# Forgetting attention of a two-layer decoder: gates projected beside the values, running sums brought back from DRAM as bias tiles, scores on each head's own 64 rows

## Chip, cores and metric

One core of one Trainium2 chip runs the whole program in one launch. The metric is the device time of one launch in microseconds (us); lower is better. Three runs of the kernel before were timed: 756.55, 757.05 and 758.76 us, median 757.05 us.

## The reference, cut to what matters

The program computes two decoder layers on 256 tokens of width 1024 in float32. Layer 0 mixes by dilated attention (three patterns), layer 1 by forgetting attention; each is followed by a SwiGLU network. The change touches layer 1's attention alone: 16 heads of 64, and for every head one gate per token, whose log-sigmoid is summed along the tokens. The difference of two sums is added to each score.

```python
def forgetting_mixer(h, w_in, b_f, w_out):
    proj = h @ w_in                                   # 3 * 1024 columns of q, k, v and 16 of gates
    ...
    log_f = jax.nn.log_sigmoid(proj[..., 3 * ATTN_WIDTH:] + b_f)
    c = lax.cumsum(log_f, axis=1)                     # 256 tokens x 16 heads
    ...
        s = jnp.einsum('bihd,bjhd->bhij', qi, k) * scale
        s = s + ci[..., None] - ck[:, :, None, :]
        s = jnp.where(key_pos[None, :] <= qpos[:, None], s, NEG_INF)
        p = jax.nn.softmax(s, axis=-1)
        return jnp.einsum('bhij,bjhd->bihd', p, vf)
    ...
    return o @ w_out
```

The term `ci` is the same for all keys of a query, and a softmax doesn't see it; the kernels add the running sum of the key alone.

## The kernel before

Every large product is made of three TensorE matmuls (`mm3`): both operands are split into a high and a low part, and high by high, high by low and low by high are summed in PSUM. The high part is a rounded copy that ScalarE (ACT) makes, the low part the difference, which VectorE (DVE) makes (`split`, L73 and L75). Weights come in pieces of 128x2048 numbers: two transfers of 512 KB each into `raw` (five buffers), issued by the queue of SyncE (SP), and two splits into `wh` and `wl` (four buffers each, by pieces). A transfer can start when DVE has split the piece five transfers earlier, and a split when TensorE (PE) is through with the piece four earlier.

The Tile scheduler fixes the order of the instructions on each engine when the program is built; at run time each engine takes its own list from the front and waits where an operand or a buffer isn't there. Two tools steer the order: `first()` raises the priority of what is within it, and a table of due work, filled by `later(i, fn, ...)` and read after each step i of the projection loop (and at its middle, i - 0.5), says at which step attention work is written down.

The attention of layer 1 works on four quads of four heads. The list `b_units` gives 12 projection steps: for a quad, q (w = 0), k (w = 1) or the values (w = 2). A step of q or k is 48 matmuls of 256 columns. The values of quads 0 and 1 are made in one pair (`proj_pair`, 512 columns a matmul), those of quad 2 beside them (`proj_tok`), and this first block is written out by hand: tokens 0 to 127 (t = 0), then tokens 128 to 255 (t = 1), whose transposed activations `norm_t` makes in the middle of the block. Then come steps 3 to 11 in a loop: q and k of quad 0 (steps 3 and 4), of quad 1 (5 and 6), and so on. For each pair of heads `scores_b` makes the scores, adds the mask, and does the softmax; `trans_b` and `pv_b` follow one or two steps later.

The gates go their own way. `gates_1` projects them with eight matmuls of 512 columns, `softplus` transposes them and starts `log1p` (about 15 small DVE instructions on 128x32 numbers, with one power on GpSimd, POOL, after the second). `gates_2` transposes the result back on PE and makes the running sum with a scan on DVE (L816). The scores get it by a longer contraction: q and k of a head lie in `qz` and `kz`, with 16 more rows (`aux`), where `kz` holds the running sums of all heads and `qz` a column that picks the head's own (`sel`, copied on POOL, L901). So the score matmuls (L832) contract over 80 or 128 rows, and `maskb` is the same for all heads.

Of the kernel before, what the change touches and what calls it, by code (L numbers as in the profile page):

```python
# [16 lines left out]
P = 128  # L17
# [14 lines left out]
def trunk(ctx: ExitStack, tc: tile.TileContext, T, out):  # L32
# [5 lines left out]
    ps = ctx.enter_context(tc.tile_pool(name="ps", bufs=1, space=bass.MemoryType.PSUM))  # L38

# [67 lines left out]

    a_units = []
# [5 lines left out]
    b_units = [(0, 2), (1, 2), (2, 2), (0, 0), (0, 1), (1, 0), (1, 1), (2, 0), (2, 1), (3, 0), (3, 1), (3, 2)]  # L114
# [650 lines left out]
    aux = (slice(64, 64 + NH), slice(0, NH))
    qz, kz = ([ap.tile([P, 2, S], F32, tag=f"fm{w}", name=f"z{w}", bufs=2) for _ in range(2)] for w in range(2))
    for y in qz[1], kz[1]:
        nc.gpsimd.memset(y[:64], 0.0)

    def gates_1():  # L770

        o = psum("o")
        for k in range(KT):
            nc.tensor.matmul(o[:32 + NH].rearrange("p (x s) -> p x s", x=2), wf[:, k, :32 + NH], xt.full[:, k],
                             start=k == 0, stop=k == KT - 1)
        z, u = gt[:NH, :S], gt[:NH, S:]
        with first():
            nc.scalar.activation(u, o[32:32 + NH, :S], AF.Copy)
            nc.vector.scalar_tensor_tensor(z, o[:NH, :S], bf, u, op0=ALU.add, op1=ALU.add)
            nc.vector.tensor_tensor(z, z, o[:NH, S:], op=ALU.add)  # L780

    def softplus():

        z = gt[:NH, :S]
        tr = psum("tr")
        for t in range(2):
            nc.tensor.transpose(tr[:, t * NH:(t + 1) * NH], z[:, t * P:(t + 1) * P], ident[:NH, :NH])
        with first():
            log1p(tr)

    def log1p(tr):
        zt, m, t, s, w, a = (ga[:, i, :] for i in range(6))
        nc.vector.tensor_copy(zt, tr[:, :2 * NH])

# [13 lines left out]
    def gates_2():  # L808

        tr = psum("tr")  # L810
        for t in range(2):
            nc.tensor.transpose(tr[:NH, t * P:(t + 1) * P], ga[:, 1, t * NH:(t + 1) * NH], ident)
        cs, one = gt[:NH, :S], gt[:NH, S:]
        with first():
            nc.vector.memset(one, 1.0)
            nc.vector.tensor_tensor_scan(cs, one, tr[:NH, :S], 0.0, op0=ALU.mult, op1=ALU.add)  # L816
            for h in range(2):
                nc.vector.tensor_copy(kz[h][aux[h]], cs[:, None, :].to_broadcast([NH, 2, S]))
# [4 lines left out]
    def scores_b(hq, pr):  # L823
# [4 lines left out]
        rows = (slice(0, 64 + NH), ALL)  # L828
        scs = [psum("sc") for _ in range(2)]
        for h in range(2):  # L830
            for qb in range(2):
                last = nc.tensor.matmul(scs[h][:, qb * P:qb * P + (qb + 1) * P],  # L832
                                        qz[h][rows[h], pr, qb * P:(qb + 1) * P],
                                        kz[h][rows[h], pr, :(qb + 1) * P], start=True, stop=True)
# [31 lines left out]
    ws = [weights("b_in", b_units[i][0] * 3 + 2) for i in range(2)]  # L866
    os = [psum("mm") for _ in range(2)]
    vs = [v_tile() for _ in range(2)]
    for i in range(2):
        bq[i][2] = vs[i]  # L870
        proj_pair(xt, ws[i], os, i, (0,))
    v_pair(vs, os[0], 0)
    w2, o2 = weights("b_in", b_units[2][0] * 3 + 2), psum("sc")
    proj_tok(xt, w2, o2[:, :S], 0, hook=(2, lambda: norm_t(*hs[1], g_b, xt, 1)))
    for i in range(2):
        last = proj_pair(xt, ws[i], os, i, (1,))
        with tc.issue_after(last.ins):
            (gates_1, softplus)[i]()
    v_pair(vs, os[1], 1)
    proj_tok(xt, w2, o2[:, S:], 1)  # L880
    bq[2][2] = v_tile(o2)
    later(4, gates_2)
    for i, (hq, w) in enumerate(b_units):
# [4 lines left out]
        if w < 2:  # L888
# [9 lines left out]
            for h in range(2):  # L898
                if w == 0:
                    pick = sel[aux[h], hq * 4 + h:hq * 4 + h + 3:2]  # L900
                    nc.gpsimd.tensor_copy(qz[h][aux[h]], pick[:, :, None].to_broadcast([NH, 2, S]))  # L901
                nc.scalar.activation((qz, kz)[w][h][own[h]], o[own[h]].rearrange("p (a b) -> p a b", a=2), AF.Copy,
                                     scale=(0.125, 1.0)[w])
# [63 lines left out]
def _constants():  # L967
# [22 lines left out]
    sel = np.zeros((80, NH), np.float32)  # L990
    sel[np.arange(NH), np.arange(NH)] = 1.0
    sel[64 + np.arange(NH), np.arange(NH)] = 1.0
# [3 lines left out]
        "maskb": np.concatenate([causal, np.zeros((P, P), np.float32), causal], 1), "sel": sel,  # L996
# [3 lines left out]
def _layout(i):  # L1000
# [31 lines left out]
    t["bf"] = np.asarray(i["b_f"])[0].reshape(NH, 1)  # L1032
# [23 lines left out]
```

## Time and profile before

| | before |
|---|---|
| median of three runs, us | 757.05 |
| span of the profiled execution, first to last instruction, us | 757.5 |
| TensorE busy, share of the span | 747.3 us, 99% |
| DVE, ACT, POOL busy | 500.0, 381.7, 56.9 us |
| DMA | 135.04 MB, mean 178 GB/s |
| first block of layer 1's attention, us from the start | 450.1 to 470.3 |
| steps 3 to 11 of its loop | 470.3 to 541.2 |

How to read it: the page gives no time of its own for the profiled execution beside its span; the span and the median agree within 0.1%. A matmul's recorded duration includes the way through the array, and the next one starts long before it ends, so what a matmul costs is the distance to the next start. The columns of a timeline are start, duration, engine, line, operation, what it writes and reads, partitions x elements, and how many were merged; in square brackets stands how long the engine had been idle and for whom.

### The profile page before, as it was taken

The numbers are of one execution on the slowest core, as the hardware profiler recorded it, in microseconds if no ns is written. First come the engines' busy times: TensorE is split into PE (matmuls) and PEld (weight loads), VectorE is DVE, ScalarE is ACT, GpSimd is POOL, SyncE is SP. The second block draws the span as 40 slices with busy tenths as digits, with TensorE's granted clock in tenths as the row PEclk, the third lists the DMA queues.
The fourth block names the chain that finished last, engine by engine and source line by source line (L and its number), as shares of the span: only waits on it lengthen the run. The fifth ranks groups of instructions, "written<-read, shape, count | busy, mean of one in ns | idle before, by whom it ended". The sixth has DMA issues, their size and how long they took to land.

```text
span 757.5 us, 14562 instructions
## 1 busy us (share of the span) xinstructions
PE 747.3 (99%) x6018; PEld 689.3 (91%) x6018; DVE 500.0 (66%) x760; ACT 381.7 (50%) x628; POOL 56.9 (8%) x99
## 2 busy tenths in 40 slices
PE   9999999999999999999999999999999999999996
PEld 7998989999988899999999988999889999999995
DVE  7987977877878466545456473887756645456533
ACT  7635437446346455444454454587645444455521
POOL 0600003004013000000000013000000000000000
PEclk9999999999999999999999999999999999999999
DMA  9965553653655267565667454634326665556601
GB/s 333 301 194 168 167 178 127 206 186 115 195 174 195 77 218 248 178 207 180 196 215 233 135 167 140 223 112 151 129 85 220 225 200 190 192 198 209 209 2 55
DMA packets 38355, 135.04 MB, mean 178 GB/s; under 512 B 4369, under 2 KB 5777, under 8 KB 38289
## 3 DMA queue, kind: packets, MB, share of 16 engines
q1 hardware_dynamic: 38144, 134.01, 53.5%
q8 instruction: 47, 0.77, 0.4%
q14 instruction: 20, 0.16, 0.1%
q10 hardware_dynamic: 144, 0.10, 0.0%
HBM read 133.05 MB, written 1.05 MB: 177 GB/s over the span
## 4 chain that ended last, share of the span: by engine, by line
PE 90%; DMA 2%; ACT 2%; issue 2%; DVE 2%; POOL 1%; SPq 0%; POOLq 0%; DVEq 0%; ACTq 0%
PE ps_mm L184 31%; PE ps_mm L179 16%; PE ps_tr L184 9%; PE ps_sc L184 7%; PE ps_o L184 7%; PE ps_tr L179 5%; PE ps_sc L179 4%; PE ps_o L179 3%; PE ps_o L284 2%; PE ps_tr L273 2%; PE ps_sc L832 1%; ACT wh L73 1%; DMA otl<-in_lead 1%; PE ps_sc L430 1%; PE ps_sc L446 1%
## 5 line engine op out<-in xcount | busy, mean ns | idle before, releaser
L73 ACT ACTIVATE wh<-raw 128x1024 fp32r<-128x1024 f32 x236 | 244.0, 1055 | 245.2 <-PE ps_mm L184 82.8
L75 DVE TENSOR_TENSOR wl<-raw,wh 128x1024 fp32r<-128x1024 f32 x236 | 285.4, 1228 | 91.3 <-ACT wh L73 91.0
L179 PE MATMUL ps_mm<-xt,wh 128*128 128x256 f32 x816 | 228.4, 280 | 1.2 <-ACT wh L73 1.2
L184 PE MATMUL ps_mm<-xt,wl 128*128 128x256 f32 x816 | 226.1, 277 | 0.0
L184 PE MATMUL ps_mm<-xt,wh 128*128 128x256 f32 x816 | 226.1, 277 | 0.0
L179 PEld LDWEIGHTS ps_mm<-xt,wh 128*128 128x128 f32 x816 | 153.4, 188 | 4.3 <-issue 2.7
L184 PEld LDWEIGHTS ps_mm<-xt,wl 128*128 128x128 f32 x816 | 153.5, 188 | 0.0
L184 PEld LDWEIGHTS ps_mm<-xt,wh 128*128 128x128 f32 x816 | 153.4, 188 | 0.1
L184 PE MATMUL ps_tr<-xt,wh 128*128 128x256 f32 x304 | 83.8, 276 | 0.0
L184 PE MATMUL ps_tr<-xt,wl 128*128 128x256 f32 x304 | 83.8, 276 | 0.0
L179 PE MATMUL ps_tr<-xt,wh 128*128 128x256 f32 x304 | 83.6, 276 | 0.0
L673 DVE TENSOR_TENSOR sa<-ps_tr,sa 128x256 f32<-128x256 f32 x38 | 16.1, 424 | 73.9 <-PE ps_tr L184 73.9
L184 PEld LDWEIGHTS ps_tr<-xt,wh 128*128 128x128 f32 x304 | 57.1, 188 | 0.0
L184 PEld LDWEIGHTS ps_tr<-xt,wl 128*128 128x128 f32 x304 | 57.1, 188 | 0.0
L179 PEld LDWEIGHTS ps_tr<-xt,wh 128*128 128x128 f32 x304 | 56.9, 188 | 0.0
L179 PE MATMUL ps_mm<-wh,xt 128*128 128x256 f32 (+1 forms) x160 | 52.9, 331 | 0.0
L184 PE MATMUL ps_mm<-wh,xt 128*128 128x256 f32 (+1 forms) x164 | 51.9, 321 | 0.0
L184 PE MATMUL ps_mm<-wl,xt 128*128 128x256 f32 (+1 forms) x164 | 51.9, 320 | 0.0
L259 POOL COPY v<-v 32x256 f32<-32x256 f32 x64 | 33.0, 516 | 138.9 <-ACT v L255 136.1
L149 POOL TENSOR_SCALAR rs<-ssq 128x1 f32<-128x1 f32 x7 | 2.2, 318 | 423.8 <-ACT junk L158 423.8
L184 PEld LDWEIGHTS ps_mm<-wl,xt 128*128 128x128 f32 x164 | 30.8, 188 | 2.6
L184 PEld LDWEIGHTS ps_mm<-wh,xt 128*128 128x128 f32 x164 | 30.5, 188 | 2.9 <-DVE xt L75 0.3
(228 smaller groups left out, 1154.1 us busy)
## 6 DMA issues: line engine op xcount, KB each, us to landing
raw<-in_gu SPq DMA_DIRECT2D x88, 512.0 KB, 4.5
raw<-in_a_in SPq DMA_DIRECT2D x68, 512.0 KB, 4.3
raw<-in_dn SPq DMA_DIRECT2D x44, 512.0 KB, 4.3
raw<-in_b_in SPq DMA_DIRECT2D x24, 512.0 KB, 4.7
raw<-in_a_out SPq DMA_DIRECT2D x8, 512.0 KB, 4.3
raw<-in_b_out SPq DMA_DIRECT2D x8, 512.0 KB, 4.7
grow<-in_norms SPq DMA_DIRECT2D x4, 512.0 KB, 5.4
x<-in_x SPq DMA_DIRECT2D x2, 512.0 KB, 5.6
```

What stands on the lines that cost most here:

```text
L73: a = nc.scalar.activation(view(hi), src, AF.Copy)
L75: return a, nc.vector.tensor_tensor(view(lo), src, view(hi).bitcast(F32), op=ALU.subtract)
L149: nc.gpsimd.tensor_scalar(m, s, rest, None, op0=ALU.add)
L179: nc.tensor.matmul(o, sh, mh, start=start, stop=False)
L184: last = nc.tensor.matmul(o[:, u], s, m[:, u], start=False, stop=end and u.stop == n)
L259: nc.gpsimd.tensor_copy(v[1 + a % 2][n:n + 32, a // 2 * S:a // 2 * S + S], by_t[a * 32:a * 32 + 32, t, g])
L273: nc.tensor.transpose(tr[:, i * P:(i + 1) * P], b, ident)
L284: nc.tensor.matmul(o[h * HD:(h + 1) * HD], v[:, c:c + HD], w(h), start=start, stop=stop)
L430: nc.tensor.matmul(scs[h][:, qb * P:qb * P + (qb + 1) * P], q[hr[h], pr, qb * P:(qb + 1) * P], k[hr[h], pr, :(qb + 1) * P], start=True, st ...
L446: nc.tensor.matmul(sc[h][c, o:o + 64], q[hr[h], pq, qb * P + a * 32:qb * P + a * 32 + 32], k[hr[h], pq].rearrange("p (b n) -> p b n", b=2) ...
L673: nc.vector.tensor_tensor(a, u, sg, op=ALU.mult)
L832: last = nc.tensor.matmul(scs[h][:, qb * P:qb * P + (qb + 1) * P], qz[h][rows[h], pr, qb * P:(qb + 1) * P], kz[h][rows[h], pr, :(qb + 1) * ...
```

## The change

The gate columns are put beside the value columns of quad 2: that piece of weights is 272 columns wide instead of 256 (its 16 gate columns split from `wf32`), it is now the first of the list, and `proj_gated` does one half of the tokens with 24 matmuls of 272 columns. The gates come out with tokens on partitions, so `gates_1` and the transposes of `softplus` fall away, and `log1p` starts after `proj_gated(1)`. The second half's `norm_t` is called at the last quarter of the pair of t = 0. `gates_2` is put at 2.5 instead of 4. Its scan is followed by two transfers that write the running sums to DRAM, and `bias` reads them back for one quad, 1536 numbers repeated on 128 partitions (768 KB); POOL then adds the causal mask to two of each head's three blocks. `scores_b` adds this tile instead of `maskb`. `qz`, `kz`, `sel` and their copies are gone: q and k of a step are copied by one ACT instruction of 128 rows, and the score matmuls contract over a head's own 64 rows, the two heads alternating.

```diff
-    b_units = [(0, 2), (1, 2), (2, 2), (0, 0), ...
+    b_units = [(2, 2), (0, 2), (1, 2), (0, 0), ...
...
-    def proj_pair(xt, w, os, half, ts=range(2)):
+    def proj_pair(xt, w, os, half, ts=range(2), hook=None):
         for t in ts:
             for k in range(half * 4, half * 4 + 4):
+                between(k, hook, last)
...
-    maskb = const("maskb", [P, 3 * P])
-    sel = const("sel", [80, NH])
+    causal = const("causal", [P, P])
...
             nc.vector.tensor_tensor_scan(cs, one, tr[:NH, :S], 0.0, op0=ALU.mult, op1=ALU.add)
-            for h in range(2):
-                nc.vector.tensor_copy(kz[h][aux[h]], cs[:, None, :].to_broadcast([NH, 2, S]))
+        for y, n in ((0, P), (P, S)):
+            nc.sync.dma_start(sums[:, y:y + n], cs[:, :n])
+
+    def bias(hq):
+        b = ap.tile([P, 12 * P], F32, tag="bias", name="bias", bufs=2)
+        nc.sync.dma_start(b, sums[hq * 4:hq * 4 + 4].rearrange("h c -> (h c)").partition_broadcast(P))
+        d = b.rearrange("p (h b j) -> p h b j", h=4, b=3)[:, :, 0:3:2]
+        nc.gpsimd.tensor_tensor(d, d, causal[:, None, None, :].to_broadcast([P, 4, 2, P]), op=ALU.add)
+        bq[hq]["bias"] = b
...
-        for h in range(2):
-            for qb in range(2):
-                last = nc.tensor.matmul(scs[h][:, qb * P:qb * P + (qb + 1) * P],
-                                        qz[h][rows[h], pr, qb * P:(qb + 1) * P],
-                                        kz[h][rows[h], pr, :(qb + 1) * P], start=True, stop=True)
+        for qb in range(2):
+            for h in range(2):
+                last = nc.tensor.matmul(scs[h][:, qb * P:qb * P + (qb + 1) * P], b[0][own[h], pr, qb * P:(qb + 1) * P],
+                                        b[1][own[h], pr, :(qb + 1) * P], start=True, stop=True)
...
-                nc.vector.tensor_tensor(s[:, :3 * P], scs[h][:, :3 * P], maskb, op=ALU.add)
+                n = (pr * 2 + h) * 3 * P
+                nc.vector.tensor_tensor(s[:, :3 * P], scs[h][:, :3 * P], b["bias"][:, n:n + 3 * P], op=ALU.add)
...
+    def proj_gated(t):
+        for k in range(KT):
+            st = both(xt, ALL, k, ALL)
+            mm3(oz[t][:, :256 + NH], [x[:, t * P:(t + 1) * P] for x in st], both(wz, ALL, k), k == 0, k == KT - 1)
+        with first():
+            nc.vector.tensor_tensor(ga[:, 0, t * NH:(t + 1) * NH], oz[t][:, 256:256 + NH], bf, op=ALU.add)
+            nc.scalar.activation(vs[2][:, t * S:(t + 1) * S], oz[t][:, :256], AF.Copy)
...
+    for t in range(2):
+        proj_gated(t)
+        if t == 1:
+            with first():
+                log1p()
+        for i in range(2):
+            hook = (6, lambda: norm_t(*hs[1], g_b, xt, 1)) if i > t else None
+            proj_pair(xt, ws[i], os, i, (t,), hook)
+        v_pair(vs[:2], os[t], t)
+    later(2.5, gates_2)
+    for hq in range(2):
+        later(3, bias, hq)
...
-            for h in range(2):
-                if w == 0:
-                    pick = sel[aux[h], hq * 4 + h:hq * 4 + h + 3:2]
-                    nc.gpsimd.tensor_copy(qz[h][aux[h]], pick[:, :, None].to_broadcast([NH, 2, S]))
-                nc.scalar.activation((qz, kz)[w][h][own[h]], o[own[h]].rearrange("p (a b) -> p a b", a=2), AF.Copy,
-                                     scale=(0.125, 1.0)[w])
+            bq[hq][w] = ap.tile([P, 2, S], F32, tag=f"fm{w}", name=f"fb{w}", bufs=2)
+            nc.scalar.activation(bq[hq][w], o.rearrange("p (a b) -> p a b", a=2), AF.Copy, scale=(0.125, 1.0)[w])
...
+                if hq < 2:
+                    later(j + 1, bias, hq + 2)
```

Where this stands in the engines' lists is decided by the scheduler. Line numbers shift by the change: `split` is L73 and L75 before, L74 and L76 after.

On PE, before, the transposes of `gates_2` (L812) stand between step 4 (`ps_mm_5450`) and step 5 (`ps_mm_5518`):

```order
L184 MATMUL ps_mm_5450<-xt_5133,wh_5234 128x256
L184 MATMUL ps_mm_5450<-xt_5133,wl_5235 128x256
L812 MATMUL ps_tr_5501<-ident_214,gates_5175 16x128 x2
L179 MATMUL ps_mm_5518<-xt_5133,wh_5377 128x256
L184 MATMUL ps_mm_5518<-xt_5133,wh_5377 128x256
```

After, they (L795) stand inside step 3 (`ps_mm_5369`), with 38 of its 48 matmuls ahead of them and 10 behind:

```order
L191 MATMUL ps_mm_5369<-xt_5136,wh_5190 128x256
L196 MATMUL ps_mm_5369<-xt_5136,wh_5190 128x256
L795 MATMUL ps_tr_5394<-ident_216,gates_5174 16x128 x2
L196 MATMUL ps_mm_5369<-xt_5136,wl_5191 128x256
L191 MATMUL ps_mm_5369<-xt_5136,wh_5190 128x256
```

Before, the 96 matmuls of steps 3 and 4 lay ahead of them; 58 of these have moved behind them.

On DVE, before, four splits of weights (L75) stand among the gates' instructions that follow the power on POOL:

```order
L798 TENSOR_SCALAR gates<-gates 128x32
L799 RECIPROCAL gates<-gates 128x32
L800 TENSOR_TENSOR gates<-gates 128x32
L801 SCALAR_TENSOR_TENSOR gates<-gates 128x32
L75 TENSOR_TENSOR wl<-raw,wh 128x1024
L802 TENSOR_SCALAR gates<-gates 128x32
L75 TENSOR_TENSOR wl<-raw,wh 128x1024
L804 SCALAR_TENSOR_TENSOR gates<-gates 128x32 x3
L75 TENSOR_TENSOR wl<-raw,wh 128x1024
L804 SCALAR_TENSOR_TENSOR gates<-gates 128x32
L75 TENSOR_TENSOR wl<-raw,wh 128x1024
L804 SCALAR_TENSOR_TENSOR gates<-gates 128x32 x3
```

After, the same stretch holds six (L76), and the scan (L799) stands behind the last two gates' instructions that follow these rows:

```order
L781 TENSOR_SCALAR gates<-gates 128x32
L782 RECIPROCAL gates<-gates 128x32
L76 TENSOR_TENSOR wl<-raw,wh 128x1024
L783 TENSOR_TENSOR gates<-gates 128x32
L76 TENSOR_TENSOR wl<-raw,wh 128x1024
L784 SCALAR_TENSOR_TENSOR gates<-gates 128x32
L785 TENSOR_SCALAR gates<-gates 128x32
L76 TENSOR_TENSOR wl<-raw,wh 128x1024
L787 SCALAR_TENSOR_TENSOR gates<-gates 128x32
L76 TENSOR_TENSOR wl<-raw,wh 128x1024
L787 SCALAR_TENSOR_TENSOR gates<-gates 128x32 x5
L76 TENSOR_TENSOR wl<-raw,wh 128x1024
```

Behind them come one more instruction of L787, the sixth split, and L788 and L789. The gates' chain is longer by two splits on DVE.

On the queue of SP, before, the 11 transfers of weights behind the norm row run through to the output weights:

```order
L86 DMA raw<-in_b_in 128x1024 x13
L55 DMA grow<-in_norms 128x1024
L86 DMA raw<-in_b_in 128x1024 x11
L86 DMA raw<-in_b_out 128x1024 x8
L86 DMA raw<-in_gu 128x1024 x6
```

After, the two writes of the sums and the four reads of bias tiles stand among them:

```order
L56 DMA grow<-in_norms 128x1024
L89 DMA raw<-in_b_in 128x1024 x6
L801 DMA sums<-v 16x128
L801 DMA sums<-v 16x256
L89 DMA raw<-in_b_in 128x1024
L806 DMA bias<-sums 128x1536 x2
L89 DMA raw<-in_b_in 128x1024 x3
L806 DMA bias<-sums 128x1536
```

The bias tiles of quads 0 and 1 stand behind a transfer of weights that can start only when DVE has split the first half of step 7's piece.

More of the change, by code (lines that the diff above doesn't have):

```diff
@@ L38, in trunk @@
     ps = ctx.enter_context(tc.tile_pool(name="ps", bufs=1, space=bass.MemoryType.PSUM))
+    dr = ctx.enter_context(tc.tile_pool(name="dr", bufs=1, space=bass.MemoryType.DRAM))
     ALL = slice(None)
@@ L81, in piece @@
         else:
-            wh, wl = (wp.tile([P, 2048], F32R, tag=y, name=y, bufs=4) for y in ("wh", "wl"))
+            wh, wl = (wp.tile([P, WIDE], F32R, tag=y, name=y, bufs=4) for y in ("wh", "wl"))
+        if key == GATED:
+            wh, wl = (y.rearrange("p (k c) -> p k c", k=KT) for y in (wh, wl))
         for c in range(2):
@@ L86, in piece @@
             nc.sync.dma_start(raw, T[key[0]][key[1]][:, u])
-            cut = lambda after=None, raw=raw, u=u: split((wh, wl), lambda y: y[:, u], raw, False, after)
+            view = lambda y, u=u: y[:, u]
+            if key == GATED:
+                raw = raw.rearrange("p (k c) -> p k c", c=256)
+                view = lambda y, c=c: y[:, c * 4:c * 4 + 4, :256]
+            cut = lambda after=None, raw=raw, view=view: split((wh, wl), view, raw, False, after)
             if todo is None:
@@ L91, in piece @@
                 todo.append(cut)
+        if key == GATED:
+            cut = lambda after=None: split((wh, wl), lambda y: y[:, :, 256:], wf32, False, after)
+            todo.append(cut)
         return wh, wl
@@ L106, in trunk @@
     qk = [(g, w) for g in range(NG) for w in range(2)]
+    WIDE = KT * (256 + NH)
+    GATED = ("b_in", 2 * 3 + 2)
     a_units = []
@@ L752, in trunk, with log1p @@
     xt, g_b = nxt["xt"], nxt["g"]
-    wf = cst.tile([P, KT, 64], F32R, name="wf")
-    nc.vector.memset(wf[:, :, NH:32].bitcast(F32), 0.0)
-    split((wf[:, :, :NH], wf[:, :, 32:32 + NH]), lambda y: y, wf32.rearrange("p (k c) -> p k c", k=KT))
     gt = v_tile()
     ga = ap.tile([P, 6, 2 * NH], F32, tag="gates", name="gates", bufs=1)
+    sums = dr.tile([NH, 3 * P], F32, name="sums")
     own = (slice(0, 64), slice(64, 128))
[L765 to L791, printed above, removed]
+    def log1p():
         zt, m, t, s, w, a = (ga[:, i, :] for i in range(6))
-        nc.vector.tensor_copy(zt, tr[:, :2 * NH])
         nc.vector.tensor_scalar(m, zt, -1.0, 0.0, op0=ALU.mult, op1=ALU.max)
@@ L864, in pv_b @@
         split(ot, lambda x: x[:, hq * 2 + pr, :], o[:, :S])
-    ws = [weights("b_in", b_units[i][0] * 3 + 2) for i in range(2)]
+    wz, oz = weights(*GATED), [psum("sc") for _ in range(2)]
+    ws = [weights("b_in", i * 3 + 2) for i in range(2)]
     os = [psum("mm") for _ in range(2)]
-    vs = [v_tile() for _ in range(2)]
-    for i in range(2):
-        bq[i][2] = vs[i]
[L871 to L882, printed above, removed]
+    vs = [v_tile() for _ in range(3)]
+    def proj_gated(t):
[5 more added lines that the diff above has]
+            nc.scalar.activation(vs[2][:, t * S:(t + 1) * S], oz[t][:, :256], AF.Copy)
+    for i in range(3):
+        bq[i][2] = vs[i]
+    for t in range(2):
[10 more added lines that the diff above has]
+        later(3, bias, hq)
     for i, (hq, w) in enumerate(b_units):
@@ L995, in _constants @@
         "mask0": m0, "mask12": m12,
-        "maskb": np.concatenate([causal, np.zeros((P, P), np.float32), causal], 1), "sel": sel,
+        "causal": causal,
     }
```

17 lines of the change are left out of this document (8 added, 9 removed).

## The prediction

> **What bounds the kernel now.** I read the page's shares and the slices first, then the chain that ended last, then the timeline of each engine between 450 and 500 us, where the change lies.
>
> ```profile
> PE 747.3 (99%) x6018; PEld 689.3 (91%) x6018; DVE 500.0 (66%) x760; ACT 381.7 (50%) x628; POOL 56.9 (8%) x99
> ...
> PE   9999999999999999999999999999999999999996
> ...
> PE 90%; DMA 2%; ACT 2%; issue 2%; DVE 2%; POOL 1%; SPq 0%; POOLq 0%; DVEq 0%; ACTq 0%
> ```
>
> TensorE (PE) is busy in every slice and carries 90% of the last chain. So each us taken off its list is a us gained, and each us in which it waits is one lost; DVE, ACT and the transfers matter only where PE waits for them. All sums are made against the profiled span, 757.5 us, 0.06% above the median of the runs (757.05).
>
> **Score matmuls: -4.1 us.** A burst of eight records (four fp32 matmuls, two passes each) of the first attention, which already contracts over 64 rows with the heads alternating (L430), and one of the second (L832), each with the row that follows:
>
> ```profile
> 143.90 0.93 PE L430 MATMUL ps_sc<-qk,qk 64*128 64x128 f32 x8
> 144.76 0.38 PE L179 MATMUL ps_mm<-xt,wh 128*128 128x256 f32 x1
> ...
> 499.47 1.48 PE L832 MATMUL ps_sc<-z,z 80*128 80x128 f32 x8
> 500.88 0.65 PE L284 MATMUL ps_o<-pt,v 128*64 128x256 f32 x4
> ...
> L832 PE MATMUL ps_sc<-z,z x64: 272/378/382, 485.0 to 540.0; 80*128 80x128 f32 x16, 80*128 80x256 f32 x16, 128*128 128x128 f32 x16, 128*128 128x256 f32 x16
> ```
>
> 144.76 - 143.90 = 0.86 us against 500.88 - 499.47 = 1.41 us for the same columns: the two heads' passes overlap on their own rows. Six bursts save 0.55; for the two followed by plain matmuls I count 0.4. Together 6 x 0.55 + 2 x 0.4 = 4.1. The bounds are 0 (no overlap) and 4.4.
>
> **First block: -1.75 us.**
>
> ```profile
> 455.70 0.39 PE L184 MATMUL ps_mm<-wh,xt 128*128 128x512 f32 x1
> 455.93 0.28 PE L184 MATMUL ps_sc<-wl,xt 128*128 128x256 f32 x1
> 456.05 0.28 PE L184 MATMUL ps_sc<-wh,xt 128*128 128x256 f32 x1
> ...
> 456.52 1.23 PE L172 MATMUL ps_tr<-ident,xn 128*128 128x128 f32 x8
> 457.51 0.36 PE L179 MATMUL ps_sc<-wh,xt 128*128 128x256 f32 x1
> ...
> 462.46 0.62 PE L774 MATMUL ps_o<-xt,wf 128*48 128x512 f32 x2
> ...
> 464.30 0.40 PE L179 MATMUL ps_mm<-wh,xt 128*128 128x512 f32 x1
> ...
> 470.30 0.28 PE L179 MATMUL ps_mm<-xt,wh 128*128 128x256 f32 x1
> ```
>
> The eight gate matmuls go (464.30 - 462.46 = 1.84), and the two transposes of `softplus` with their change of shape, some 0.3. The 48 matmuls of 256 columns (0.12 us each) get a sixteenth more: +0.36. By the new list and these distances, from 450.07: 24 of 272 columns 3.0, 18 of 512 (0.23) 4.1, the transposes 1.0, 6 of 512 1.4, 24 of 272 3.0, and 0.1 at each of four changes: the gates of t = 1 are complete at **462.9**; then 24 of the pair, 5.6, end the block at 468.55 instead of 470.30. The transposes of `norm_t` have 1.4 us of matmuls between them and their reader, in place of 18 x 0.12 = 2.2; should the splits on ACT and DVE need the longer time, PE waits up to 0.8. I count nothing, since the reader needs the first half first. The extra split of the gate columns (128x128 numbers, an eighth of a weight split) falls 13 transfers ahead, under PE's matmuls of the network before.
>
> **The gates' chain: PE waits 6.2 us.** This is the term that decides.
>
> ```profile
> 467.47 0.19 DVE L793 COPY gates<-ps_tr 128x32 f32<-128x32 f32 x1 [0.26 <-PE ps_tr L787]
> ...
> 468.19 5.43 POOL L797 TENSOR_TENSOR gates<-euler,gates 128x32 f32<-128x32 f32 x1 [12.66 <-DVE gates L796]
> ...
> 473.65 0.18 DVE L798 TENSOR_SCALAR gates<-gates 128x32 f32<-128x32 f32 x1 [5.54 <-POOL gates L797]
> ...
> 474.59 1.22 DVE L75 TENSOR_TENSOR wl<-raw,wh 128x1024 fp32r<-128x1024 f32 x1
> 475.72 0.17 DVE L802 TENSOR_SCALAR gates<-gates 128x32 f32<-128x32 f32 x1
> ...
> 480.77 0.19 DVE L806 TENSOR_TENSOR gates<-gates 128x32 f32<-128x32 f32 x1
> ...
> 481.19 0.38 PE L812 MATMUL ps_tr<-ident,gates 128*16 128x128 f32 x2
> 483.16 0.67 DVE L816 TENSOR_TENSOR_SCAN v<-v,ps_tr 16x256 f32<-16x256 f32 x1
> ```
>
> Before, the chain runs from 467.47 to 480.96, with 5.43 us of power on POOL during which DVE stands, and four weight splits of 1.13 us among the rest; PE reaches its transposes at 481.19, just after. After, it starts at 463.1 (462.9 and 0.2 to DVE). The power starts 0.72 later as before (463.8) and returns to DVE at 469.3; the rest took 480.96 - 473.65 = 7.3 and gets two splits more, 2.3: **478.9**, on PE 479.1. PE reaches the transposes after 38 matmuls of step 3; the 96 matmuls from 470.30 to 481.19 took 0.1134 each, so at 468.55 + 4.3 = **472.9**. DVE and PE keep their lists' order, so PE stands 479.1 - 472.9 = 6.2 us, with steps 3 and 4 queued behind. The last split among the gates needs a transfer issued when the first is done, at 471.1; the transfers of `b_in` land after a median of 4.7 (row below), so its ACT split ends near 477, before DVE comes to it at 477.3.
>
> **A wait that goes: -0.7 us.**
>
> ```profile
> 483.22 1.06 ACT L73 ACTIVATE wh<-raw 128x1024 fp32r<-128x1024 f32 x1 [2.36 <-DMA raw<-in_b_in]
> 484.31 1.21 ACT L902 ACTIVATE z<-ps_mm 64x512 f32<-64x512 f32 x2
> ...
> 484.95 1.58 PE L832 MATMUL ps_sc<-z,z 80*128 80x128 f32 x8 [0.63 <-ACT z L902]
> ```
>
> The copy of k stood behind a split that waited for its transfer. With PE 6 us late those transfers are in; I count the wait as gone, with its 0.1 of waking.
>
> **The clock after the hole: +2.85 us.** No wait inside the kernel is longer than 1 us, but its ends show what a longer one does.
>
> ```profile
> 0.87 4.21 PE L293 MATMUL ps_o<-mhalf 128*128 128x256 f32 x10 [0.87 <-POOL euler L68]
> 4.73 2.05 PE L366 MATMUL ps_sc<-wh,xt 128*128 128x512 f32 x4
> 6.58 0.67 PE L366 MATMUL ps_sc<-wl,xt 128*128 128x512 f32 x2
> 7.09 1.08 PE L366 MATMUL ps_sc<-wh,xt 128*128 128x512 f32 x4
> 8.01 0.62 PE L366 MATMUL ps_sc<-wl,xt 128*128 128x512 f32 x2
> ...
> 749.92 0.28 PE L184 MATMUL ps_tr<-wh,al 128*128 128x256 f32 x1
> ...
> 753.00:754.00 1.00, 0.00 (x0) 0.00 (x0) 0.62 (x2) 0.74 (x2) 0.00 (x0) 1.00 0.00 0
> 754.00:755.00 1.00, 0.00 (x0) 0.00 (x0) 0.00 (x0) 0.00 (x0) 0.00 (x0) 0.59 0.71 236
> ```
>
> In the last two rows (windows) the column behind the five engines is the granted clock: the last matmul ends at 750.2, and the clock falls in the slice from 754.0, 4 us later. At the start four matmuls take 6.58 - 4.73 = 1.85 us, from 7.09 on 0.92: half speed for 5.7 us after the first at 0.87. A hole of 6.2 us is longer than those 4, so I take the start's price, half of 5.7. The bounds are 0 and 2.85. [...]
>
> **The way through DRAM: 0 to +2.6, taken as 0.**
>
> ```profile
> raw<-in_b_in SPq DMA_DIRECT2D x24, 512.0 KB, 4.7
> ...
> xw<-in_lead SPq DMA_DIRECT2D x1, 768.0 KB, 8.3
> out<-xn SPq DMA_DIRECT2D x2, 256.0 KB, 2.0
> ...
> sel<-in_sel SPq DMA_DIRECT2D x1, 5.0 KB, 4.9
> ...
> L901 POOL COPY z<-sel x8: 603/605/1164, 220.6 to 523.6; 16x512 f32<-16x512 f32 x8
> ```
>
> Scan 479.3 to 480.2; the sums' writes are issued by 480.6 and land after 2.0 (`out`) to 4.9 (`sel`). Ahead of the bias tiles stands a transfer that waits until DVE has split step 7's first half, which ACT can split only when step 3 is done: 482 at half clock, so that split ends at 484.4 and the first tile is issued at 484.8. Landing takes 6 to 8.3 us (768 KB; I take 6.2, since only one transfer is ahead): 491. POOL's add reads two inputs of 1024 elements, four times the elements of L901's copy: 2.4 us, 493.6; the two adds of the scores, 1.0, end at 494.6. Who waits: the second burst of scores, whose PSUM buffers these adds free. At half clock PE comes to it at 479.1 + 2.85 + 10 and 72 matmuls (9.3) + 0.3 + a burst 1.0 + 24 matmuls 2.75 = 495.3, so 0; without the half clock at 492.5, and with the chain 0.9 us earlier a wait of 1.3. By the long ends (4.9, 8.3, POOL 3.1) it is 497.9: +2.6. DVE stands at the add meanwhile, but the splits of steps 7 and 8 are ahead of it. [...] The later tiles are fetched over 8 us ahead of their use, and the one copy per step in place of two (L902) saves ACT time that no one waits for: 0; so do POOL's copies, which ran under PE's matmuls.
>
> **Sum:** -4.1 - 1.75 - 0.7 + 6.2 + 2.85 + 0 = +2.5 us, a span of 760.0; against the median 757.05 this is **759.5 us** (+0.33%).
>
> **Rivals.** B, the clock stays: the 2.85 goes and the bias wait of 1.3 comes, +0.95, 758.0 us. For it: 6.2 is not far above 4. C, the bias tile takes the long ends: +2.5 + 2.6, 762.1 us; for it speaks that small transfers behind others took 4.9. D, on the other side: the hole on PE is short. Should the gates be through on DVE by 475.9, a hole of 3 us, shorter than the 4 that lowered the clock, remains: -6.55 + 3 + 1.0 for the bias tile, which still comes about 14 us after the gates, = -2.5, 754.5 us, and without any hole -5.5, 751.5; faster from a hole of 3.2 down. Against it stand the 5.43 of POOL and DVE's fixed list. E, the heads' passes don't overlap and the 4.1 isn't had: 763.6; against it stands L430, of the same shapes.
>
> **How the numbers follow.** Chances: forecast 0.45, B 0.15, C 0.16, D 0.20, E 0.04. A measurement of this kernel tells 0.3%, 2.3 us, from no change: 754.8 to 759.3 is the same. The forecast lies at that edge, half to each side (0.22 and 0.23). Faster 0.20 (D); same 0.22 + 0.15 = 0.37; slower 0.23 + 0.16 + 0.04 = 0.43. The forecast's own range is 758.0 to 761.0. The range of 8 in 10 leaves out half of D and the far part of C and E: 753.5 to 762.5.
>
> **What would show it.** Right: PE idle for about 6 us inside step 3 ahead of L795, released by DVE's gates; a granted clock below 1 in the 6 us behind it; bursts of L822 0.86 us apart from what follows; block one at 18.5 us. Wrong: L795 reached less than 3 us ahead of the gates, a clock that stays at 1.00, or a wait above 2 us ahead of the second burst of L822, released by DVE's adds behind POOL's L808.

## The result: 0.3% slower, and the profile after

| | before | after |
|---|---|---|
| median of six runs, us | 756.91 (756.55 to 758.76) | 759.38 (758.91 to 760.37) |
| profiled execution: span, us | 757.5 | 757.5 |
| profiled execution: own time, us | not given | 759.32 |
| TensorE busy, us | 747.3 | 743.0 |

The ratio of the times is 1.003, with a 95% interval of 1.0019 to 1.0040: between 1.4 and 3.0 us slower. The page of the changed kernel, its shares and its slices (40 slices of 18.9 us):

```profile
PE 743.0 (98%) x6008; PEld 684.8 (90%) x6008; DVE 500.8 (66%) x756; ACT 374.8 (49%) x620; POOL 60.5 (8%) x93
...
PE   9999999999999999999999998899999999999996
...
PEclk9999999999999999999999999899999999999999
```

TensorE is busy for 4.3 us less, and yet the kernel is longer. Two slices hold an 8 where before every slice held a 9, and one slice has a granted clock below full speed. All of it lies between 454 and 493 us (the 25th and 26th slice). The timeline of PE there, and the waits of PE between 440 and 545 us (line, whom it waited for, us in total, times, longest):

```profile
448.39 0.29 PE L191 MATMUL ps_sc<-wh,xt 128*128 128x272 f32 x1
...
466.43 0.29 PE L191 MATMUL ps_mm<-xt,wh 128*128 128x256 f32 x1
...
470.63 0.28 PE L196 MATMUL ps_mm<-xt,wh 128*128 128x256 f32 x1
476.61 0.60 PE L795 MATMUL ps_tr<-ident,gates 128*16 128x128 f32 x2 [5.70 <-DVE gates L789]
476.86 0.56 PE L196 MATMUL ps_mm<-xt,wl 128*128 128x256 f32 x1
...
488.86 0.93 PE L822 MATMUL ps_sc<-fb,fb 64*128 64x128 f32 x8
489.72 0.39 PE L191 MATMUL ps_mm<-xt,wh 128*128 128x256 f32 x1
...
502.67 0.93 PE L822 MATMUL ps_sc<-fb,fb 64*128 64x128 f32 x8
503.52 0.87 PE L298 MATMUL ps_o<-pt,v 128*64 128x256 f32 x8
...
540.73 0.65 PE L298 MATMUL ps_o<-pt,v 128*64 128x256 f32 x4
```

```profile
PE ps_tr L795 <- DVE gates L789: 5.7, 1, 5.7
```

The last matmul of the 38 starts at 470.63, the gates' transposes at 476.61, and there is no other wait of PE in the whole stage. A burst of scores and the row behind it are 503.52 - 502.67 = 0.85 us apart, where they were 1.41. The granted clock in windows of 1 us (the column behind the five engines):

```profile
474.00:475.00 1.00, 0.00 (x0) 0.00 (x0) 1.00 (x2) 0.02 (x1) 0.00 (x0) 1.00 0.93 250
475.00:476.00 1.00, 0.00 (x0) 0.00 (x0) 1.00 (x2) 0.00 (x0) 0.00 (x0) 0.70 0.91 356
...
481.00:482.00 1.00, 1.00 (x7) 1.00 (x6) 0.80 (x2) 0.70 (x1) 0.00 (x0) 0.50 0.01 1
482.00:483.00 1.00, 1.00 (x10) 1.00 (x10) 0.96 (x1) 0.00 (x0) 0.00 (x0) 0.88 0.26 70
```

A mean of 0.70 between 1.00 and 0.50 puts the fall at 475.4, and 0.88 puts the return at 482.2: PE works at half speed from 476.6 to 482.2. The gates' chain on DVE and POOL, and the first bias tile:

```profile
461.11 0.17 DVE L867 TENSOR_TENSOR gates<-ps_sc,bf 128x16 f32<-128x16 f32 x1 [2.67 <-PE ps_sc L196]
...
467.27 0.18 DVE L781 TENSOR_SCALAR gates<-gates 128x32 f32<-128x32 f32 x1 [5.54 <-POOL gates L780]
...
476.36 0.19 DVE L789 TENSOR_TENSOR gates<-gates 128x32 f32<-128x32 f32 x1
...
491.70 1.01 DVE L828 TENSOR_TENSOR p<-ps_sc,bias 128x384 f32<-128x384 f32 x2
```

```profile
461.81 5.43 POOL L780 TENSOR_TENSOR gates<-euler,gates 128x32 f32<-128x32 f32 x1 [7.89 <-DVE gates L779]
488.16 5.86 POOL L808 TENSOR_TENSOR bias<-bias,causal 128x1024 f32<-128x1024 f32 x2 [20.92 <-DMA bias<-sums]
```

DVE stands 5.54 us for the power, then works through the gates with six weight splits among them, 9.3 us until 476.55. Of the two POOL rows merged here, the first took 2.53 us and the second 3.37.

For a stage by stage account, two rows of before that were not shown yet, the first matmul of the attention and the first behind its last burst of scores:

```profile
450.07 0.39 PE L179 MATMUL ps_mm<-wh,xt 128*128 128x512 f32 x1
...
540.35 0.87 PE L284 MATMUL ps_o<-pt,v 128*64 128x256 f32 x8
```

| stage, by starts on PE | before | after | difference | predicted |
|---|---|---|---|---|
| first block (450.07 to 470.30; 448.39 to 466.43) | 20.23 | 18.04 | -2.2 | -1.75 |
| step 3 to the first burst (to 484.95; to 488.86) | 14.65 | 22.43 | +7.8 | 6.2 + 2.85 - 0.7 = +8.35 |
| first burst to the row behind the last (to 540.35; to 540.73) | 55.40 | 51.87 | -3.5 | -4.1 |
| sum | 90.28 | 92.34 | +2.1 | +2.5 |

The stage accounts for +2.1 us, inside the interval of the runs. That the spans of both profiles are equal has another cause, far ahead of the change. The first burst of scores of the first attention:

```profile
47.41 0.93 PE L430 MATMUL ps_sc<-qk,qk 64*128 64x128 f32 x8
```

```profile
45.95 0.92 PE L444 MATMUL ps_sc<-qk,qk 64*128 64x128 f32 x7
```

Before's profiled execution came to it 1.46 us later, and 1.68 us later to the attention of layer 1. In the other profiles of this study, nearly all of kernels with the change, the same burst lies anywhere between 46.3 and 47.7 us, so this is how the start happens to go, not the change.

### The profile page after: what moved, and what is told of

It reads as the page before. It is cut to its first block, busy times and chain, and to the rows that moved or that the text cites. A ratio compares the mean times of both kernels' runs of the same rounds, so it can differ in the third digit from the quotient of the medians.

```text
span 757.5 us, 14517 instructions
## 1 busy us (share of the span) xinstructions
PE 743.0 (98%) x6008; PEld 684.8 (90%) x6008; DVE 500.8 (66%) x756; ACT 374.8 (49%) x620; POOL 60.5 (8%) x93
## 4 chain that ended last, share of the span: by engine, by line
PE 90%; issue 3%; ACT 2%; DVE 2%; DMA 2%; POOL 1%; SPq 0%; POOLq 0%; ACTq 0%; DVEq 0%
PE ps_mm L196 31%; PE ps_mm L191 16%; PE ps_tr L196 9%; PE ps_sc L196 8%; PE ps_o L196 7%; PE ps_tr L191 5%; PE ps_sc L191 4%; PE ps_o L191 3%; PE ps_o L298 2%; PE ps_tr L287 2%; ACT wh L74 1%; PE ps_sc L822 1%; PE ps_sc L444 1%; DMA otl<-in_lead 1%; PE ps_sc L460 1%
## 5 line engine op out<-in xcount | busy, mean ns | idle before, releaser
L74 ACT ACTIVATE wh<-raw 128x1024 fp32r<-128x1024 f32 x236 | 243.9, 1055 | 251.3 <-PE ps_mm L196 88.2
L76 DVE TENSOR_TENSOR wl<-raw,wh 128x1024 fp32r<-128x1024 f32 x236 | 287.7, 1238 | 90.1 <-ACT wh L74 89.9
```

Source lines behind the costliest of these rows:

```text
L74: a = nc.scalar.activation(view(hi), src, AF.Copy)
L76: return a, nc.vector.tensor_tensor(view(lo), src, view(hi).bitcast(F32), op=ALU.subtract)
```

## The experiments

The theory: the score matmuls and the block save about 6 us, as the trace says, and the hole ahead of the gates' transposes together with the half clock behind it takes 8.5 us back. The rivals: the way of the sums through DRAM is what costs; the clock has another reason; the scores' saving isn't real. Each kernel was timed beside the kernel before on the same chip, so ratios to before are compared; the changed kernel has 1.0030.

### 1. The power on POOL taken out

```diff
-        nc.gpsimd.tensor_tensor(t, euler.to_broadcast([P, 2 * NH]), t, op=ALU.pow)
+        nc.gpsimd.memset(t, 0.5)
```

> The changed kernel, with the power on POOL (128x32 numbers, 5.43 us) replaced by a constant fill, so the gates' exponential is left out; all engines' lists stay as they are. Theory (the hole on PE and the half clock behind it eat the gain): the gates reach PE some 5 us earlier, at about 471.6, and PE comes at 470.6, so a hole of 1 us or less is left, the clock stays at 1.00, and the time falls by 4.8 + 2.7 us, less up to 1.3 us of waiting for the bias tile: 752 to 753.5 us. Rival 1 (the sums' way through DRAM is what costs): the tile's path is only 5 us earlier while PE is 7.5 us earlier, so a wait of 2 us or more appears ahead of the second burst of scores, and the time stays above 754. Rival 2 (the half clock has nothing to do with the hole): the slow stretch stays and the time is about 754.6 us.

Measured: 752.72 us median (before 757.38), ratio 0.9953 (0.9935 to 0.9970). The transposes on PE:

```profile
470.90 0.39 PE L795 MATMUL ps_tr<-ident,gates 128*16 128x128 f32 x2 [0.37 <-DVE gates L789]
```

In this profile the hole is 0.4 us and the clock stays at 1.00 around it. The second burst took 1.31 us in place of 0.96, all that was left of a late bias tile. Three of the twelve runs took 755.1 to 759.5 us at a mean granted clock of 0.994 to 0.996 (the other nine 0.997 to 0.999); no trace of these three was kept, so where the clock fell in them is open. With the hole away the change is 0.5% faster than before: the first rival fell in this form, and the clock followed the hole.

### 2. The hole filled with idle work

```diff
+        o = psum("o")
+        for _ in range(12):
+            nc.tensor.matmul(o[:, :256], mhalf.to_broadcast([P, P]), mhalf.to_broadcast([P, 256]), start=True, stop=True)
         tr = psum("tr")
...
-    later(2.5, gates_2)
...
-                proj_feat(xt, wt, o[:, c * S:(c + 1) * S], c)
+                proj_feat(xt, wt, o[:, c * S:(c + 1) * S], c, (5, gates_2) if i == 3 and c == 1 else None)
```

> The changed kernel, with 12 fp32 matmuls of 256 columns (0.43 us each by the pairs at the start, 5.1 us together) put right ahead of the gates' transposes, where PE would stand; the gates' chain is the same, and PE gives back no work earlier. Theory (the idle stretch itself halves the clock): PE is busy but for under 1 us, the granted clock stays at 1.00, and the half-speed stretch of 2.7 us goes: 756.7 us, or up to 758 if the bias tile now comes late by 1.3 us. Rival (the slow matmuls behind the hole come from late weights or from traffic): 759.4 us, with the slow stretch still there.

Measured: 757.47 us (before 757.38), ratio 1.0003 (0.9994 to 1.0012). PE, and the windows of 2 us:

```profile
471.68 5.38 PE L795 MATMUL ps_o<-mhalf 128*128 128x256 f32 x24
477.42 0.39 PE L798 MATMUL ps_tr<-ident,gates 128*16 128x128 f32 x2 [0.35 <-DVE gates L789]
```

```profile
476.00:478.00 2.00, 1.65 (x11) 1.14 (x10) 1.49 (x4) 0.00 (x0) 0.00 (x0) 1.00 1.01 340
```

The gates come no earlier, but the clock stays at 1.00 and the time falls by 2.0 us against the changed kernel (1.0030 - 1.0003, of 757). Counted from the start of the block, the first burst came 2.7 us earlier than in the changed kernel, as the price of the half clock says. Behind it 0.7 is lost again: half of that in the second burst, to which PE now comes sooner than its bias tile (1.31 us in place of 0.96), the rest in the stretches beside it. So the half clock is a cost of its own, and it goes with the idle stretch: 0.50 where PE stood for 5.7 us, 1.00 where the same stretch was filled.

### 3. The scores on 64 rows alone, in the kernel before

```diff
-        for h in range(2):
-            for qb in range(2):
+        for qb in range(2):
+            for h in range(2):
...
-                                        qz[h][rows[h], pr, qb * P:(qb + 1) * P],
-                                        kz[h][rows[h], pr, :(qb + 1) * P], start=True, stop=True)
+                                        qz[h][own[h], pr, qb * P:(qb + 1) * P],
+                                        kz[h][own[h], pr, :(qb + 1) * P], start=True, stop=True)
```

> The kernel before, with one part of the change alone: the score matmuls contract over a head's own 64 rows, the two heads alternating. The running sums are still made and copied beside k but no longer reach the scores, so the forgetting term is left out of the result. Theory (the two heads' passes overlap): eight bursts shorter by 0.4 to 0.55 us, 756.9 - 4.1 = 752.8 us. Rival (no gain in the scores, since something behind each burst takes it back): 756 to 757 us.

Measured: 754.34 us (before 757.38), ratio 0.9960 (0.9948 to 0.9972), -3.0 us.

```profile
497.32 0.93 PE L832 MATMUL ps_sc<-z,z 64*128 64x128 f32 x8
498.17 0.87 PE L284 MATMUL ps_o<-pt,v 128*64 128x256 f32 x8
```

The saving is real, 0.55 us a burst, but 4.1 was too much: the first burst here still takes 1.40 us, because the second head's copy of k comes late, and the stretches between the bursts grow by 0.4 us in all.

### 4 and 5. What makes the burst short

One kernel does both blocks of one head and then both of the other; one keeps the order and reads rows 0 to 63 for both heads.

```diff
-        for qb in range(2):
-            for h in range(2):
+        for h in range(2):
+            for qb in range(2):
```

> The changed kernel, but each burst does both blocks of one head and then both of the other, instead of alternating. Theory (the gain comes from neighbours in the list that sit on different rows): only the pair in the middle of a burst overlaps, a burst takes about 1.2 to 1.4 us instead of 0.86, and the time is 759.4 + 8 x 0.35 to 8 x 0.5, 762 to 763.5 us. Rival (64 rows in place of 80 or 128 is what saves): bursts stay at 0.86 us and the time at 759.4 us.

```diff
-                last = nc.tensor.matmul(scs[h][:, qb * P:qb * P + (qb + 1) * P], b[0][own[h], pr, qb * P:(qb + 1) * P],
-                                        b[1][own[h], pr, :(qb + 1) * P], start=True, stop=True)
+                last = nc.tensor.matmul(scs[h][:, qb * P:qb * P + (qb + 1) * P], b[0][own[0], pr, qb * P:(qb + 1) * P],
+                                        b[1][own[0], pr, :(qb + 1) * P], start=True, stop=True)
```

> The changed kernel, but the score matmuls of both heads of a pair read rows 0 to 63 of q and k, so the odd heads' scores are left out (they get those of the even ones). The number, the length and the order of the matmuls stay. Theory A (what was gained comes from two neighbours that sit on different rows and run side by side): bursts go back to about 1.4 us and the time to 759.4 + 6 x 0.55 + 2 x 0.4 = 763.5 us. Theory B (a matmul of 64 rows is short by itself, whatever its neighbour): bursts stay at 0.86 us and the time at 759.4 us.

Measured: heads one after the other 760.24 us, ratio 1.0036 (1.0024 to 1.0048), not to be told from the changed kernel; same rows 764.38 us, ratio 1.0096 (1.0083 to 1.0110), 5.0 us above it. A burst and the row behind it, first with one head after the other, then with the same rows:

```profile
503.53 0.93 PE L822 MATMUL ps_sc<-fb,fb 64*128 64x128 f32 x8
504.39 0.87 PE L298 MATMUL ps_o<-pt,v 128*64 128x256 f32 x8
```

```profile
503.34 1.57 PE L822 MATMUL ps_sc<-fb,fb 64*128 64x128 f32 x8
504.85 0.65 PE L298 MATMUL ps_o<-pt,v 128*64 128x256 f32 x4
```

0.86 us and 1.51 us. Both my theory of the first (neighbours must alternate) and its rival (64 rows are short by themselves) fell; together the two runs leave one reading. The heads' matmuls run side by side where they lie on different rows (0.86 us a burst) and not where they share them (1.51), and they need not be neighbours in the list: in the single records of experiment 4 the second head's first pass starts 13 ns after the first head's (6 ns in the changed kernel), although two matmuls of the first head stand ahead of it in the list.

### 6. The gates' transposes back behind step 4

```diff
-    later(2.5, gates_2)
+    later(4, gates_2)
     for hq in range(2):
-        later(3, bias, hq)
+        later(4, bias, hq)
```

> The changed kernel with the gates' transposes put behind step 4, where they stood before, the bias tiles right behind them, and the second burst of scores half a step later. PE comes to the transposes at 476.8, the gates are there at 476.6: no hole there, and the clock stays. The bias tile is then late instead: scan to 478.3, sums landed 481.8, tile landed 486.9, masked 489.6, first adds done 490.5, while PE comes to the second burst at 486.1: a wait of 4.4 us there. If that is too short to lower the clock, 759.4 - 5.7 - 2.7 + 4.4 = 755.4 us; if it lowers it, 758.1 us. Rival (the way through DRAM is hidden, so the place inside step 3 was the whole fault): no wait, 751 us.

Measured: 761.01 us (before 757.26), ratio 1.0050 (1.0038 to 1.0062). PE and then the clock:

```profile
494.51 1.01 PE L822 MATMUL ps_sc<-fb,fb 64*128 64x128 f32 x3 [6.34 <-DVE p L828]
```

```profile
492.00:493.00 1.00, 0.00 (x0) 0.00 (x0) 0.00 (x0) 0.00 (x0) 1.00 (x1) 0.93 0.93 311
...
499.00:500.00 1.00, 1.00 (x8) 1.00 (x7) 0.96 (x2) 0.60 (x4) 0.00 (x0) 0.66 0.97 406
```

The hole has moved: no wait at the gates, but 6.3 us ahead of the second burst, with the half clock behind it. I had expected 4.4 and 758.1 with the clock lowered. From the transposes to POOL's first addition it took 491.43 - 478.53 = 12.9 us, where I had counted 10.1. So the way through DRAM is not hidden for its own sake: in the changed kernel it hides behind the hole and the half clock.

### 7 and 8. The logarithm in two halves, first try

```diff
+        with first():
+            done = log1p(t, True, t == 1)
...
+            if t == i == 0:
+                with first():
+                    log1p(0, False, True)
...
-        wt = weights("b_in", hq * 3 + w)
+        wt = weights("b_in", hq * 3 + w, done if i < 6 else None)
```

The second of the two has, besides, the transposes at the end of step 3:

```diff
-    later(2.5, gates_2)
+    later(3, gates_2)
```

> The changed kernel with the logarithm of the gates made in two halves of 128x16 numbers, the first while PE is still at the pair of t = 0, and with four weight splits held back on DVE until the second half is through; the transposes stand after 24 matmuls of step 3. The power of the second half should take half of 5.43 us, so the gates are through at 461.8 + 2.7 + 2.9 + 2 splits = 469.8, while PE comes at 468.7: a hole of 1 us, clock at 1.00, the bias tile masked at about 483, ahead of the second burst at 484: 759.4 - 4.7 - 2.7 = 752 us, 753 with small waits. That beats the kernel before by 0.6%. Rival (the power's time doesn't depend on the number of elements, or two transfers of weights in front of the bias tile make it late): 755 us or more.

> As the one before, with the transposes at the end of step 3 (48 matmuls ahead of them). PE comes at 471.4, the gates are through by 469.8: no hole at all, but the sums start 1.6 us later, and the bias tile is masked at about 485 while PE comes to the second burst at 483.2: a wait of up to 2 us there instead of 1 us at the gates: 751.5 to 753 us.

Measured: 760.56 us, ratio 1.0039 (1.0025 to 1.0052), and 764.15 us, ratio 1.0093 (1.0078 to 1.0108), with before at 757.26. Both expectations fell. The waits of PE in the first of the two, its DVE, and its clock in four windows:

```profile
PE ps_sc L196 <- DVE xt L76: 2.9, 1, 2.9
PE ps_sc L830 <- DVE p L836: 2.5, 1, 2.5
PE ps_tr L803 <- DVE gates L797: 0.3, 1, 0.3
```

```profile
460.15 0.17 DVE L789 TENSOR_SCALAR gates<-gates 128x16 f32<-128x16 f32 x1 [2.80 <-POOL gates L786]
...
462.42 0.68 DVE L76 TENSOR_TENSOR xt<-ps_tr,xt 128x512 fp32r<-128x512 f32 x1
```

```profile
463.00:464.00 1.00, 0.85 (x5) 0.85 (x6) 1.00 (x5) 0.00 (x0) 0.00 (x0) 0.75 0.00 0
...
466.00:467.00 1.00, 1.00 (x6) 1.00 (x6) 0.00 (x0) 0.00 (x0) 0.00 (x0) 0.54 0.06 16
...
494.00:495.00 1.00, 1.00 (x7) 0.83 (x7) 1.00 (x5) 0.60 (x3) 1.00 (x1) 0.61 1.03 414
...
497.00:498.00 1.00, 1.00 (x8) 1.00 (x7) 1.00 (x5) 1.00 (x3) 0.00 (x0) 0.68 0.45 98
```

The hole at the gates is gone (0.3), as expected, but the first half's instructions stood on DVE ahead of the split of the second half's activations (462.42), and they waited 2.80 us for the power. PE waited 2.9 us in the block for that split, and the clock fell; the gates came late, so the tile did, and a second wait of 2.5 us lowered the clock again. In the other kernel the first wait was the same 2.9 us and the second 5.2, and the clock fell at both. The twelve runs of the first kernel go from 757.3 us at a mean granted clock of 0.998 to 762.5 us at 0.992: one kernel with one list of work lost the clock in some runs and kept it in at least one. The last section comes back to that.

### 9, 10 and 11. The splits out of the chain, and the power in halves behind nothing

The rest of the logarithm is put behind two splits that are ready while POOL works; the next four are put behind the scan (for two of them the splitting is written down later). In the second kernel the power of each half is started as soon as its gates are there, and the rest is done once for both; the third also reads and masks the bias tiles by pairs of heads.

```diff
+        with tc.issue_after(state["cut"].ins):
+            nc.vector.tensor_scalar(s, t, 0.5, 1.0, op0=ALU.mult, op1=ALU.add)
...
+        for cut in state.pop("held"):
+            cut(scan)
...
             with first():
+                power(1)
                 log1p()
...
+        if t == 0:
+            with first():
+                power(0)
```

> The changed kernel with the weight splits kept out of the gates' chain: two stand on DVE ahead of the instruction that waits for the power (so they run while POOL works), the other four behind the scan. The power stays whole, 5.43 us; the transposes stand after 24 matmuls of step 3. Gates through at 461.8 + 5.5 + 15 instructions of 0.2 = 470.2, PE there at 468.7: a hole of 1.6 us, clock at 1.00; scan 471.5, sums landed 475, tile landed 480, masked 483, ahead of the second burst at 485. 759.4 - 4.1 - 2.7 = 752.6 us, 0.6% below the kernel before. Rival (the tile is late again, since transfers of weights stand in front of it): 755 us or more, with a wait of over 2 us ahead of the second burst.

> As the one before, with the power in two halves of 128x16: the first is started while the pair of t = 0 runs and nothing on DVE waits for it until the second is done. The second takes 2.9 us as in the run of the halves, so the gates are through at 461.8 + 2.9 + 3 = 467.7, ahead of PE at 468.7: no hole; scan 469.7, tile masked at 482, second burst at 483.3: 751 us. Rival (the first half's power on POOL slows DVE's split of the second half's activations, and PE waits at the second half's first matmul): 753 us or more, with that wait ahead of the second half.

> As the one before, with each bias tile read and masked by pairs of heads (two transfers of 384 KB, two additions on POOL of half the size), so that the first pair's half is there 1 to 2 us earlier. If the one before has no wait ahead of the second burst, the time is the same, 751 us; if it has one, it is shorter here by 1 to 2 us.

Measured, with before at 758.51 on this chip: 754.96 us, ratio 0.9956 (0.9942 to 0.9970); 753.09 us, ratio 0.9936 (0.9923 to 0.9949); 753.68 us, ratio 0.9939 (0.9927 to 0.9952). All three beat both kernels, each by 0.15 to 0.2% less than I had expected (752.6 and 751 us are ratios of 0.994 and 0.992). The first, PE's wait and DVE:

```profile
PE ps_tr L799 <- DVE gates L793: 1.3, 1, 1.3
```

```profile
463.52 2.45 DVE L76 TENSOR_TENSOR wl<-raw,wh 128x1024 fp32r<-128x1024 f32 x2 [0.47 <-ACT wh L74]
468.59 0.18 DVE L785 TENSOR_SCALAR gates<-gates 128x32 f32<-128x32 f32 x1 [2.62 <-POOL gates L783]
```

The second, PE's only wait between 440 and 545 us, and DVE:

```profile
PE ps_sc L832 <- ACT fb L914: 0.4, 1, 0.4
```

```profile
465.63 0.18 DVE L788 TENSOR_SCALAR gates<-gates 128x32 f32<-128x32 f32 x1
...
483.94 1.02 DVE L838 TENSOR_TENSOR p<-ps_sc,bias 128x384 f32<-128x384 f32 x2 [2.27 <-POOL bias L818]
```

With the splits alone moved a hole of 1.3 us is left, with the clock at 1.00; with the power in halves there is none, and the first addition of a tile (483.94) is done ahead of the second burst, at 485.07. So there was nothing for the tiles by pairs to shorten, and they didn't; in the profile of that kernel PE waits 2.2 us for ACT where the second waits 0.4, and why is open.

## Why the prediction was right, by its steps

- **What decides:** the hole, the half clock behind it, and a saving of about 6 us that they outweigh. Experiments 1, 2, 9 and 10 show it from four sides. The forecast's case came, with +2.1 us in the trace and +2.5 in the medians against +2.5.
- **Score matmuls, -4.1:** -3.5 measured. The bursts shrink by 3.8 (0.37, 0.17 and six times 0.55; the second of them by less than I counted), and the stretches between them give 0.3 back. The cause that the prediction gave, passes that overlap on the heads' own rows, held (experiment 5); that the heads must alternate, my addition in experiment 4, did not.
- **First block, -1.75:** -2.2. Some 0.2 of the rest are the transposes of `norm_t`, which take 0.79 us instead of 0.99.
- **The chain, 6.2:** 476.61 less 470.74, when a matmul behind the 38th could have started, is 5.9. With the block begun 1.68 us earlier, the chain was to start at 461.4 and end at 477.2, with PE there at 471.2; it started at 461.1 and ended at 476.55, with PE there at 470.7.
- **The wait for k, -0.7:** 24 matmuls of 0.1134 fill 2.7 of the 3.6 us ahead of before's first burst; 0.9 went.
- **The clock, +2.85:** the 82 matmuls from 476.86 on took 12.0 us instead of 9.3, and the transposes 0.1 more: 2.8. The half price was right, but that the size agrees this closely is luck: experiment 5 has the same hole of 5.7 us and paid 1.8 (last section). I had read the 5.7 us of half speed at the start from distances alone; the granted clock's column shows 1.00 there. The condition was wrong: I took 4 us of standing as what it needs. Experiment 7 lowered the clock with waits of 2.9 and 2.5 us, so rival D's hole of 3 us, which was to keep the clock, might well have lost it. Experiment 9's 1.3 us kept it, and so did a wait of 1.2 us at 29 us in the kernel before, where I had written that no wait inside it is longer than 1 us.
- **The way through DRAM, 0:** the second burst took 0.96 us, 0.1 more than the others, so 0 was right, but by luck, since two errors cancelled. The single rows of the first tile fit the sizes taken: it landed after 6.0 us (taken 6.2), and POOL's addition took 2.53 (taken 2.4). But it was issued at 482.0, 1.1 us sooner than the forecast moved by 1.68 says (483.1); and a weight split on DVE stood 3.12 us beside POOL's addition, so the adds of the scores began at 491.70, 1.0 us after the tile was masked (490.69). There was no reserve: the first adds ended at 492.7 and PE came at 492.65. Without the half clock I had a wait of 1.3 there; experiments 1 and 2 show that burst 0.45 longer. Where the gates lie later against PE's list, experiments 6 and 8 show 6.3 and 5.2 us at the same place.
- **The base:** I set the sum against the span of before and called it 0.06% off the median. In every run of the changed kernel the time is 1.8 us above its span (759.32 against 757.5), in the runs of before beside the experiments too (758.51 against 756.7), and before's profiled execution started 1.5 us late; so its span belongs to a time of some 759.3 us (estimate, 757.5 + 1.8), not to the median. The span of 760.0 was therefore wrong by 2.5 us while the time was right, since the time used the difference alone.

## What to carry to other kernels

Here a wait of some us on TensorE cost its length and could cost half of a slow stretch behind it as well (5.9 us did in the changed kernel, 2.9 and 2.5 in experiment 7, 1.3 in experiment 9 did not), so lay each new chain beside the moment at which that engine comes to its end before counting what a change saves. Then look at what the late engine does meanwhile: here DVE stood 5.5 us for POOL with splits in hand and did them afterwards, inside the chain that PE waited for, and the same work in another order turned +0.3% into -0.4%, with the power in two halves into -0.6%. An instruction that waits for another engine should have nothing urgent behind it in its list: in experiment 7 DVE stood 2.80 us for POOL with a split behind it, and PE stood 2.9 us for that split.

## What the hardware showed that was not expected

- **The clock fell after shorter waits than I took.** By the windows of 1 us the half-speed stretches lasted 463.5 to 466.9 and 494.2 to 497.6 in experiment 7 (3.4 us each, with waits of 2.9 and 2.5 us), 475.4 to 482.2 in the changed kernel and 492.9 to 499.7 in experiment 6 (6.8 each, with waits of 5.7 and 6.3). In both of experiment 7's the clock fell some 0.4 us after PE had begun to work again, in the changed kernel 1.2 us before. Some distances fit each other: the two falls of experiment 7, at 463.50 and 494.22, are 30.72 us apart, nine times 3.41, which is the length of its half-speed stretches; in the changed kernel, by windows of 0.1 us, half speed lasted 6.83 us (475.41 to 482.24) and the full speed that followed 273.07 (to the fall at 755.30, behind the last matmul), 40 times as long. That every change lies on such a step is not shown. Behind the last matmul of the thirteen profiles the clock fell after anything between 2.0 us (experiment 9) and 4.8 us (experiment 3), with 4.0 in the kernel before (750.2 to 754.2) and 4.7 in the changed one (750.6 to 755.3); the 4 us of the prediction were one such draw. The price varied too. In experiment 5, with the same hole:

```profile
477.03 0.59 PE L795 MATMUL ps_tr<-ident,gates 128*16 128x128 f32 x2 [5.70 <-DVE gates L789]
...
480.00:481.00 1.00, 1.00 (x8) 1.00 (x8) 0.29 (x1) 1.00 (x2) 0.00 (x0) 0.77 0.72 285
```

  The clock is back at 480.6 (0.72 in this window), so PE works at half speed for 3.5 us behind the hole in place of 5.6, a price of 1.8 us (estimate, half of 3.5). The first burst, at 488.26, comes 11.23 us after the start of the transposes, 1.0 less than the 12.25 of the changed kernel, as this says. If the stretch was as long as the 6.83 us there, the clock fell at 473.7, 3.3 us ahead of the hole's end (estimate). That experiment 7's runs spread for the same reason is likely but not shown, since one trace of it was kept.
- **POOL's additions and some of DVE's instructions took longer beside each other.** In the changed kernel a split and a pair of scalings on DVE that overlap with POOL's additions:

```profile
488.66 3.12 DVE L76 TENSOR_TENSOR wl<-raw,wh 128x1024 fp32r<-128x1024 f32 x1 [0.20 <-ACT wh L74]
...
498.82 2.77 DVE L839 TENSOR_SCALAR p<-p,c_b 128x256 f32<-128x256 f32 x2
```

  A split takes 1.24 us on average and this pair of scalings 0.60 elsewhere (495.10); one POOL addition takes 2.40 (499.04), and the second of the first two, which began while the split was still there, took 3.37. DVE's adds of the scores, which read PSUM and the bias tile, were not slowed beside it (491.70, two in 1.01 us, as at 505.85 with POOL idle), nor were two splits beside the power (experiment 9, 2.45 us from 463.52). What the slowed instructions have in common is not shown.
- **A power of half the elements took about half the time:** 2.91 and 2.90 us for the two halves of 128x16 in experiment 10 against 5.43 for 128x32, so starting a first piece early cost 0.4 us of POOL's time in all.
